# Regrouping the per-head matmuls of dilated attention between projection runs

## The chip, the cores and the metric

The kernel runs on one core of one Trainium2 chip. The metric is device time of one execution in microseconds; the median of several runs counts. The core's engines work side by side: TensorE (PE; its weight loads are PEld), VectorE (DVE), ScalarE (ACT), GpSimd (POOL) and SyncE (SP), which only issues DMAs here. Each takes its own instructions in order and waits on semaphores for the others.

## What is computed

A two-layer trunk over 512 tokens of width 1024: a state-space layer with its MLP, then an attention layer with its MLP. The change touches the attention alone. Sixteen heads of 64 have three branches each (window 128 at dilation 1, 512 at 4, 2048 at 16), and the outputs of the branches are mixed by the softmax of their log-sums. That mix equals one softmax over the keys of all three branches together, and so the kernel computes it.

```python
kv = (u @ w_kv).reshape(bsz, seq, 2, N_BRANCHES, N_HEADS, HEAD_DIM)
q = (u @ w_q).reshape(bsz, seq, N_BRANCHES, N_HEADS, HEAD_DIM)
for i, (win, dil) in enumerate(DILATED_BRANCHES):
    s = jnp.einsum('brnqhe,brnkhe->brnhqk', qb, k_band) * (HEAD_DIM ** -0.5)
    s = jnp.where(band_mask(nb, span), s, NEG)
    p = jnp.exp(s - max(s)); den = sum(p)
    o_i = einsum(p, v_band) / den; lse_i = max(s) + log(den)
o = sum_i softmax_i(lse)[i] * o_i
y = o @ w_o
```

## The kernel before

**Pairs and blocks.** Heads are taken in 8 pairs, a pair's queries in 4 blocks `qb` of 128. For one block TensorE does three small pieces of work. `attn_scores` (matmuls on L1107 and L1115) makes the scores of both heads in two PSUM buffers of the tag `aux`: 192, 384, 448 or 512 columns wide for blocks 0 to 3. Behind it stands the softmax: mask and maximum on VectorE (L1122, L1124), exponential on ScalarE (L1126), reciprocal and normalising on VectorE (L1129, L1131). `attn_turn` transposes the probabilities (L1142, L1144) and copies them to SBUF on both engines (L1147 to L1151). `attn_out` multiplies them by the values (L1163, L1170) into the pair's output tile `po`, which VectorE copies out when the pair is done (L1390).

**Projections as filler.** The q, k and v projections of later pairs, and a part of the output projection, come from a generator `feed`. Each step is three matmuls of 512 columns (L827, L828, L829: weights and activations are split in a high and a low part), or, for the values of the dilated branches, three of 256 columns (L1253 to L1255). A step yields its budgeted time: 0.64 us for three matmuls of 512 columns, 0.327 for the half as wide, 0.1 for a transpose. `fill(t)` runs steps until the budget t is used. One pair of q and k projections is KQ = 30.72, four heads' values are V = 32.77 (V counts 16 transposes, the generator makes 8). So `per`, a twelfth of what a pair takes from the feed, is 2.56 in even pairs and 5.29 in odd ones, 1.59 in pair 6 and 1.07 in pair 7. AHEAD is how far the feed is ahead of the heads when they begin, LEFT what stays for pair 7, REST what stays behind it.

**Order.** The order on TensorE is the program's order (`self.pinned(nc.tensor)`); on VectorE and ScalarE a planner places instructions by its own estimate of when they are ready, and each engine then runs them in that order. Per block the program has: transposes of this block, a fill of 1.4 per, scores of the next block, a fill of 1.6 per, value products of this block, and at once the transposes of the next.

**What else runs.** Weight blocks come by DMA three ahead. `weights` splits each in two halves: a cast on ScalarE (L799) and a subtraction on VectorE (L801), which, while heads run, are placed behind the exponential and the normalising pass of the latest scores in the program. In the first four pairs a gating job runs per block: `late_step` finishes the job at hand and issues four DMAs of 256 KB for the next, `late_half` does the next one's first half (L1494, then L1501). `split_o` splits a finished pair's output for the output projection (L1310, L1311), tied behind the same two passes.

Of the kernel before, what the change touches and what calls it, by code (L numbers as in the profile page):

```python
# [16 lines left out]
KT = D // P  # L17
# [15 lines left out]
PUMPS_END = ((0, 3), (1, 0), (1, 3))  # L33


AHEAD, LEFT, REST = 12.2, 11.6, 4.5

PARTS, PARTS_END = (1.4, 1.6, 0.0), (1.0, 1.0, 1.0)
NEG = -1e30


# [53 lines left out]
class Trunk:  # L95
# [1078 lines left out]
    def attention(self, adaq, adakv, gate):  # L1174
# [10 lines left out]
        kqs, vs, oparts = [None] * KT, [None] * 4, []  # L1185
# [119 lines left out]
        def split_o(k, cs=slice(0, T)):  # L1305
            if not any(uo):
                self.uo_tiles = self.uz_tiles()
            parts = [self.uo_tiles[k % 4][:, k // 4 * 2 + i] for i in range(2)]
            oh, ol = [x[:, cs] for x in parts]
            i = nc.scalar.copy(oh, ow[k][:, cs])  # L1310
            j = nc.vector.tensor_tensor(ol, ow[k][:, cs], oh.bitcast(F32), ALU.subtract)  # L1311

            self.after(i.ins, self.act_mark)
            self.after(j.ins, self.mark)
            uo[k] = parts
# [34 lines left out]
        def fill(t):  # L1350
            state[0] += t
            while state[0] > 0:
                c = next(steps, None)
                if c is None:
                    state[0] = 0.0
                    return
                state[0] -= c

        KQ, V = 6 * 8 * 0.64, 16 * 0.64 + 16 * 0.1 + 64 * 0.327
        with self.pinned(nc.tensor):  # L1360
            fill(0.327 * 15.5)
            self.pumped()
            self.table(AF.Exp, self.act_mark)
            fill(KQ + V + AHEAD - 9 * 0.64 - 0.327 * 15.5)
            self.heads = True
            nxt = self.attn_scores(0, kqs[0][0])
            fill(9 * 0.64)
            for pair in range(KT):

                per = (KQ + V * (pair % 2) - LEFT * (pair == KT - 2) if pair < KT - 1 else  # L1370
                       4 * 7 * 0.64 + LEFT - AHEAD - REST) / 12
                po = self.mm_ps()
                parts = PARTS if pair < KT - 1 else PARTS_END
                for qb in range(4):
                    pts = self.attn_turn(qb, nxt, kqs[pair][1])
                    fill(per * parts[0])
                    self.late_half()
                    if qb < 3:
                        nxt = self.attn_scores(qb + 1, kqs[pair][0])
                    elif pair < KT - 1:  # L1380
                        nxt = self.attn_scores(0, kqs[pair + 1][0])
                    fill(per * parts[1])
                    self.attn_out(pair, qb, pts, vs[pair // 2], po)

                    end = pair == KT - 1
                    if qb == 3 or end and qb == 2:
                        if ow[pair] is None:
                            ow[pair] = self.t([P, T], f"h{pair}")
                        bs = slice(3 if end and qb == 3 else 0, qb + 1)
                        nc.vector.tensor_copy(ow[pair].rearrange("p (b i r) -> p b r i", b=4, r=4)[:, bs],  # L1390
                                              po.rearrange("p (b r i) -> p b r i", b=4, r=4)[:, bs])
                        if end:
                            split_o(pair, slice(bs.start * P, bs.stop * P))
                    fill(per * parts[2])
                    self.late_step()
            fill(1000)
        self.heads = False
        self.table(AF.Sqrt, self.act_mark)
# [391 lines left out]
```

## Time and profile before

| what | us |
|---|---|
| median of 3 runs | 1551.63 (1550.26 to 1555.54) |
| the profiled execution's own time | 1551.77 |
| its span, first to last instruction | 1550.0 |
| TensorE matmuls busy over the span | 1464.0 (94%) |
| VectorE busy | 943.3 (61%) |
| ScalarE busy | 569.5 (37%) |
| the stretch of the attention heads | 694 to 1155 |

TensorE's matmuls are pipelined, so its busy share overstates how full it is: the distance from one start to the next start is the better measure, and the projections' 0.23 us is its steady state. In the rows below L12 is line 12 of the program and the arrow in brackets names what an engine waited for.

### The profile page before, as it was taken

To read this page: it belongs to the slowest core of one execution; us is meant where nothing else is said; L and a number is where in the kernel's file an instruction comes from. 1 tells how busy PE (TensorE), PEld (TensorE's weight loads), DVE (VectorE), ACT (ScalarE), POOL (GpSimd) and SP (SyncE) were. 2 spreads that over 40 slices of the span, in tenths; PEclk is the share of its full clock that TensorE was granted. 3 is DMA by queue.
4 is the path that set the end of the run, shared out by engine and by line. 5 is a ranking of instruction groups with operands and counts; after the bars stand their busy time and mean duration, and the time that the engine had idled before them with its cause. 6 is when DMAs were issued, how large, how long until landed. Compare 5 with 4: busy or idle time off the path is not lost. (4 is left out here: it accounts for less than half of the span.)

```text
span 1550.0 us, 27063 instructions
## 1 busy us (share of the span) xinstructions
PE 1464.0 (94%) x11540; PEld 1225.2 (79%) x11540; DVE 943.3 (61%) x1643; ACT 569.5 (37%) x990; POOL 134.1 (9%) x112
## 2 busy tenths in 40 slices
PE   2666999999999999999999999999999999999998
PEld 2445789888888888987987887898778888888887
DVE  8989996889884345635656756533558434344332
ACT  5566633413243233523322332332445423232222
POOL 8867200000000000100000000000000000000000
PEclk9687999999999999999999999999999999999999
DMA  9412580976643323233444445222334233232301
GB/s 219 147 56 78 159 254 28 301 242 204 208 159 109 108 88 123 59 107 114 138 126 142 139 116 157 71 67 56 116 104 137 82 109 108 83 109 82 109 1 55
DMA packets 214488, 188.59 MB, mean 122 GB/s; under 512 B 7480, under 2 KB 208352, under 8 KB 214368
## 3 DMA queue, kind: packets, MB, share of 16 engines
q1 hardware_dynamic: 214368, 186.87, 39.8%
q8 instruction: 90, 1.47, 0.4%
q14 instruction: 30, 0.25, 0.1%
HBM read 182.66 MB, written 4.19 MB: 121 GB/s over the span
## 5 line engine op out<-in xcount | busy, mean ns | idle before, releaser
L799 ACT CAST W<-W 128x1024 fp32r<-128x1024 f32 (+1 forms) x228 | 223.6, 1031 | 392.9 <-PE mm L828 201.8
L829 PE MATMUL mm<-uz,W 128*128 128x512 f32 (+1 forms) x952 | 358.1, 377 | 2.8 <-DVE W L801 2.8
L828 PE MATMUL mm<-uz,W 128*128 128x512 f32 (+1 forms) x952 | 357.8, 376 | 2.8 <-DVE uz L749 2.5
L827 PE MATMUL mm<-uz,W 128*128 128x512 f32 (+1 forms) x952 | 359.9, 380 | 0.2 <-ACT uz L1310 0.2
L801 DVE TENSOR_TENSOR W<-W,W 128x1024 fp32r<-128x1024 f32 (+1 forms) x228 | 266.6, 1197 | 151.1 <-ACT W L799 127.4
L827 PE MATMUL mm<-hid,W 128*128 128x512 f32 (+1 forms) x792 | 298.7, 378 | 0.9 <-ACT hid L1000 0.6
L828 PE MATMUL mm<-hid,W 128*128 128x512 f32 (+1 forms) x792 | 296.1, 374 | 2.7 <-DVE hid L1001 2.7
L829 PE MATMUL mm<-hid,W 128*128 128x512 f32 (+1 forms) x792 | 295.4, 373 | 0.0
L829 PEld LDWEIGHTS mm<-uz,W 128*128 128x128 f32 x952 | 179.7, 189 | 35.8 <-DVE W L801 3.2
L828 PEld LDWEIGHTS mm<-uz,W 128*128 128x128 f32 x952 | 179.7, 189 | 35.0 <-DVE uz L749 2.9
L827 PEld LDWEIGHTS mm<-uz,W 128*128 128x128 f32 x952 | 179.5, 189 | 34.0 <-ACT uz L1310 0.6
L828 PEld LDWEIGHTS mm<-hid,W 128*128 128x128 f32 x792 | 149.2, 188 | 29.4 <-DVE hid L1001 3.8
L827 PEld LDWEIGHTS mm<-hid,W 128*128 128x128 f32 x792 | 148.8, 188 | 28.8 <-issue 1.4
L829 PEld LDWEIGHTS mm<-hid,W 128*128 128x128 f32 x792 | 149.0, 188 | 26.6
L852 DVE SCALAR_TENSOR_TENSOR h<-mm,ada,h 128x512 f32<-128x512 f32 (+1 forms) x77 | 54.1, 708 | 148.4 <-PE mm L829 148.3
L1501 DVE SCALAR_TENSOR_TENSOR aacc<-W,cs,aacc 128x256 f32<-128x256 f32 x196 | 95.5, 487 | 4.0
L1029 DVE TENSOR_TENSOR sg<-sg 128x512 f32<-128x512 f32 x64 | 43.8, 688 | 55.5 <-ACT uz L1028 55.4
L1027 ACT ACTIVATE sg<-mm 128x512 f32<-128x512 f32 x60 | 35.6, 595 | 113.6 <-PE mm L829 112.0
L1253 PE MATMUL mm<-W,hid 128*128 128x256 f32 x256 | 73.5, 287 | 0.0
L1254 PE MATMUL mm<-W,hid 128*128 128x256 f32 x256 | 72.4, 283 | 0.0
L1255 PE MATMUL mm<-W,hid 128*128 128x256 f32 x256 | 72.4, 283 | 0.0
L1126 ACT ACTIVATE sg<-aux,st 128x192 f32<-128x192 f32 (+3 forms) x64 | 36.7, 577 | 96.1 <-DVE st L1124 96.1
(329 smaller groups left out, 1700.6 us busy)
## 6 DMA issues: line engine op xcount, KB each, us to landing
W<-in_mlp_w_dram SPq DMA_DIRECT2D x64, 1024.0 KB, 5.4
W<-in_ada_w_dram SPq DMA_DIRECT2D x20, 1024.0 KB, 7.2
h<-in_ada_w_dram SPq DMA_DIRECT2D x64, 256.0 KB, 3.2
W<-in_w_kv_dram SPq DMA_DIRECT2D x12, 1024.0 KB, 5.3
W<-in_w_kv_dram SPq DMA_DIRECT2D x24, 512.0 KB, 4.3
W<-in_attn_w_q_dram SPq DMA_DIRECT2D x24, 512.0 KB, 5.8
W<-in_ssm_w_glu_dram SPq DMA_DIRECT2D x16, 512.0 KB, 5.8
W<-in_kv_ada_w_dram SPq DMA_DIRECT2D x8, 1024.0 KB, 5.6
```

The source lines that it names most:

```text
L799: h = (nc.gpsimd.tensor_copy if first else nc.scalar.copy)(wh[:, ks], raw[:, ks])
L801: j = eng.tensor_tensor(wl[:, ks], raw[:, ks], wh[:, ks].bitcast(F32), ALU.subtract)
L827: nc.tensor.matmul(o, wh[:, k], uh, start=(start and k == order[0]), stop=False)
L828: nc.tensor.matmul(o, wh[:, k], ul, start=False, stop=False)
L829: self.pe_mark = nc.tensor.matmul(o, wl[:, k], uh, start=False, stop=(stop and k == order[-1])).ins
L852: self.mark = nc.vector.scalar_tensor_tensor(self.h[k][:, cs], src[:, cs], gate[:, k:k + 1], self.h[k][:, cs], ALU.mult, ALU.add).ins
L1029: nc.vector.tensor_tensor(rl, rl, rl, ALU.mult)
L1126: self.act_mark = nc.scalar.activation(p[:, 0:W], ps[:, 0:W], AF.Exp, bias=st[:, 1, e:e + 1], scale=0.125, accum_out=st[:, 2, e:e + 1]).ins
L1253: nc.tensor.matmul(ps[:, j], us[0], wh, start=(k == 0), stop=False)
L1254: nc.tensor.matmul(ps[:, j], us[0], wl, start=False, stop=False)
L1255: nc.tensor.matmul(ps[:, j], us[1], wh, start=False, stop=(k == KT - 1))
L1501: i = nc.vector.scalar_tensor_tensor(acc, raw[k], self.cs[:, k:k + 1], acc, ALU.mult, ALU.add)
```

## The change

The order of the three pieces is regrouped. Behind the scores of a block no longer stands one projection run, then its transposes. The loop now has groups: value products of block qb, transposes of block qb + 1, scores of block qb + 2, one behind the other with no projections between, then one fill and, at its end, `late_half`. `late_step` moves from behind the value products and their fill to right behind the scores. A pair has five groups: three with a fill of 3.2 per (the third without scores), then the value products of block 3 with the copy of `po` and the next pair's scores 0 (1.2 per), then the next pair's transposes 0 and scores 1 (1.2 per). Pair 6 has parts of its own (2.6, 2.6, 2.6, 2.1, 2.1), pair 7 has four groups. Before the loop pair 0 gets its first transposes, scores 1 and a fill of three steps. AHEAD goes from 12.2 to 15.0 and LEFT from 11.6 to 14.4, so `per` of pair 6 becomes 1.36 and that of pair 7 stays 1.07.

```diff
-AHEAD, LEFT, REST = 12.2, 11.6, 4.5
-PARTS, PARTS_END = (1.4, 1.6, 0.0), (1.0, 1.0, 1.0)
+AHEAD, LEFT, REST = 15.0, 14.4, 4.5
+PARTS, PARTS_6, PARTS_END = (3.2, 3.2, 3.2, 1.2, 1.2), (2.6, 2.6, 2.6, 2.1, 2.1), (3.2, 3.2, 3.2, 2.4, 0.0)
...
                 po = self.mm_ps()
-                parts = PARTS if pair < KT - 1 else PARTS_END
-                for qb in range(4):
-                    pts = self.attn_turn(qb, nxt, kqs[pair][1])
-                    fill(per * parts[0])
-                    self.late_half()
-                    if qb < 3:
-                        nxt = self.attn_scores(qb + 1, kqs[pair][0])
-                    elif pair < KT - 1:
-                        nxt = self.attn_scores(0, kqs[pair + 1][0])
-                    fill(per * parts[1])
-                    self.attn_out(pair, qb, pts, vs[pair // 2], po)
+                parts = PARTS if pair < KT - 2 else PARTS_6 if pair < KT - 1 else PARTS_END
+                if pair == 0:
+                    pts = self.attn_turn(0, nxt, kqs[0][1])
+                    nxt = self.attn_scores(1, kqs[0][0])
+                    fill(3 * 0.64)
+                for qb in range(5):
+                    if qb < 4:
+                        self.attn_out(pair, qb, pts, vs[pair // 2], po)
...
-                    fill(per * parts[2])
-                    self.late_step()
+                    if qb < 3:
+                        pts = self.attn_turn(qb + 1, nxt, kqs[pair][1])
+                    elif qb == 4 and not end:
+                        pts = self.attn_turn(0, nxt, kqs[pair + 1][1])
+                    if qb < 2:
+                        nxt = self.attn_scores(qb + 2, kqs[pair][0])
+                    elif qb > 2 and not end:
+                        nxt = self.attn_scores(qb - 3, kqs[pair + 1][0])
+                    if qb < 4:
+                        self.late_step()
+                    fill(per * parts[qb])
+                    if qb != 3:
+                        self.late_half()
```

## Rows read from the trace of the kernel before

**Rows 1.** Windows: length, busy us of PE, PEld, DVE, ACT, POOL, clock, DMA, GB/s.

```profile
693.00:1155.00 462.00, 455.97 (x5629) 376.96 (x5628) 256.63 (x608) 152.23 (x304) 0.00 (x0) 1.00 0.37 110
55.20:57.00 1.80, 1.80 (x16) 0.40 (x8) 1.80 (x1) 0.00 (x0) 1.50 (x1) 0.50 0.00 0
59.90:60.30 0.40, 0.40 (x12) 0.13 (x4) 0.36 (x2) 0.40 (x2) 0.40 (x1) 1.00 0.98 366
```

**Rows 2.** Waits of TensorE, 690 to 1160 us: total us, times, longest.

```profile
PE aux L1142 <- DVE sg L1131: 5.1, 5, 1.6
PE mm L828 <- DVE uz L1311: 0.4, 1, 0.4
PE mm L827 <- ACT W L1277: 0.3, 1, 0.3
PE mm L827 <- ACT uz L1310: 0.2, 1, 0.2
```

**Rows 3.** Timeline, TensorE, an undisturbed block: start, us, engine, line, operation, count.

```profile
799.02 0.39 PE L829 MATMUL mm<-uz,W 128*128 128x512 f32 x1
799.34 0.71 PE L1107 MATMUL aux<-W 64*128 64x128 f32 x8
...
800.58 0.50 PE L827 MATMUL mm<-hid,W 128*128 128x512 f32 x1
800.92 0.39 PE L828 MATMUL mm<-hid,W 128*128 128x512 f32 x1
801.15 0.39 PE L829 MATMUL mm<-hid,W 128*128 128x512 f32 x1
...
809.65 0.66 PE L1163 MATMUL mm<-W,W 128*64 128x128 f32 x8
...
811.78 0.47 PE L827 MATMUL mm<-uz,W 128*128 128x512 f32 x1
812.09 0.39 PE L828 MATMUL mm<-uz,W 128*128 128x512 f32 x1
```

**Rows 4.** Timeline, VectorE, four places: idle before and what ended it in brackets.

```profile
861.15 0.35 DVE L1494 TENSOR_SCALAR aacc<-h,cs 128x256 f32<-128x256 f32 x1 [1.81 <-DMA h<-in_ada_w_dram]
...
1112.50 2.36 DVE L801 TENSOR_TENSOR W<-W,W 128x1024 fp32r<-128x1024 f32 x2 [2.51 <-PE aux L1115]
...
1125.53 0.55 DVE L1131 TENSOR_SCALAR sg<-sg,st 128x192 f32<-128x192 f32 x2
...
1157.11 0.29 DVE L1311 TENSOR_TENSOR uz<-h,uz 128x128 fp32r<-128x128 f32 x1 [0.36 <-ACT uz L1310]
```

**Rows 5.** Timeline, TensorE, around pair 7's blocks 0 and 1.

```profile
1123.29 0.50 PE L827 MATMUL mm<-uz,W 128*128 128x512 f32 x1
...
1126.73 0.50 PE L828 MATMUL mm<-uz,W 128*128 128x512 f32 x1 [0.37 <-DVE uz L1311]
...
1131.85 0.50 PE L827 MATMUL mm<-uz,W 128*128 128x512 f32 x1
...
1135.33 0.38 PE L1142 MATMUL aux<-cst,sg 128*64 128x128 f32 x2
```

**Rows 6.** Timeline, TensorE, a block whose transposes wait.

```profile
866.12 0.66 PE L1163 MATMUL mm<-W,W 128*64 128x128 f32 x8
...
868.69 0.41 PE L1142 MATMUL aux<-cst,sg 128*128 128x128 f32 x2 [1.22 <-DVE sg L1131]
...
869.51 0.47 PE L827 MATMUL mm<-hid,W 128*128 128x512 f32 x1
```

**Rows 7.** Line 1494's waits, a gating job's first instruction: us, times.

```profile
  DMA h<-in_ada_w_dram: 42.3, 14
```

**Rows 8.** Instructions by line and shape: count, busy us, mean ns, idle before.

```profile
L1390 DVE COPY h<-mm 128x512 f32<-128x512 f32 x7 | 7.5, 1076 | 6.9 <-PE mm L1170 6.9
```

**Rows 9.** Timeline, TensorE, the same sixteen matmuls at either clock.

```profile
54.57 2.79 PE L282 MATMUL aux<-h,aacc 128*32 128x384 f32 x16
...
59.26 1.50 PE L282 MATMUL aux<-uz,aacc 128*32 128x384 f32 x16
```

## The prediction

> **What bounds the kernel now.** I read four views in this order. The windows say which engine is full and at which clock: over the attention heads, 693 to 1155 us, TensorE is busy 456 of 462 us at a granted clock of 1.00 (2.4 GHz), while VectorE is busy 257 and ScalarE 152 [rows 1]. So a microsecond is saved here only if TensorE starts its next matmul sooner. The amount of matmul work does not change; what can change is (a) the time TensorE waits for another engine and (b) the seams between unlike matmuls. For (a), TensorE's waits over that stretch [rows 2] are to be read as a list of everything that can be won: the transposes waited 5 times, 5.1 us in all, for the normalised probabilities, and 0.9 us went on three waits for copies and casts. No wait for a weight load or a weight split is among them. For (b), the timeline of an undisturbed block [rows 3] shows what a seam costs. For what makes the waits, the timeline of VectorE [rows 4] shows who stood ahead of the softmax in its queue.
>
> The heads run from a step budget: `fill(F)` issues projection steps of 0.64 (three matmuls) until F is used up. A step takes 3 x 0.23 = 0.68 us [rows 3], so a fill of F lasts about 1.06 F.
>
> **The waits that are there.** A block's chain is: scores, mask and maximum, exponential, normalising, transposes. Counted from the first projection behind the scores, undisturbed, it takes 2.7 us for block 0 (1123.29, to the end of the first half of the pass at 1125.53, and a start) and 3.5 us for block 1 (1131.85 to 1135.33) [rows 4, 5]; for block 3, with twice the columns or more, I take 4.2, an estimate from the same reading. Before, in an even pair (per = 2.56), the cover is 1.6 per plus the value products, 4.4 + 1.3 us (866.12 to 868.69 less 1.22 idle [rows 6]). That is enough unless something stands ahead on VectorE, and something does: the gating jobs' first instruction sat for its DMA 14 times, 42.3 us in all, 3.0 each [rows 7], and one of these at 861.15 is behind the wait at 868.69 [rows 4, 6]. In pair 6 it is a weight split that waited for the scores to release its buffer (1112.50), and that took 2 x 1.22 us ahead of block 3's maximum. So the 6.0 us are queueing on VectorE. Counted from start to start they are more, because each wait also costs a restart: the stalled group takes 869.51 - 866.12 = 3.39 us and the free one 811.78 - 809.65 = 2.13, which is 1.26 for 1.22 of idling [rows 3, 6]. The eight places together come to 6.9 us so counted.
>
> **Part 1: longer cover inside a pair.** Scores are now two groups ahead of their value products, and a fill of 3.2 per stands between scores and their transposes. Even pairs: 1.06 x 8.2 + 0.2 + 1.3 = 10 us against 4.2 needed; odd pairs 19; pair 7 (per 1.07): 5.1. A VectorE delay of 3 us no longer reaches TensorE in pairs 0 to 5. This removes 3.4 us of waits there (pair 0 block 3, pair 2 blocks 2 and 3); those of pairs 6 and 7 I also count as removed here, 3.5 us, and charge what comes back below. Sum **-6.9**.
>
> **Part 2: fewer seams.** A projection run pays at its ends: 0.09 for entering small matmuls (799.34 - 799.02 = 0.32 against 0.23), 0.11 for leaving scores (800.58 to 800.92) and 0.08 for leaving transposes (811.78 to 812.09), the latter mostly overlapped with the transposes, so I take 0.03 [rows 3]. A pair had eight runs and has five. Saved: three or four entries (0.3 us), three exits from transposes (0.1), one change from products to transposes (about 0.15). Added: three changes from transposes to scores and one from products to scores, which no row shows. The nearest is the entry to scores from full-height projections, 0.09; below it zero, above it 0.17, that of products to transposes. Taken: 0.09 x 3 + 0.15. Net 0.15 per pair, x7 = 1.0 (-0.9 to +3.4), and about 0.5 in pair 7, which goes from ten runs to four. Sum **-1.5** (+0.5 to -4).
>
> **Part 3: what is moved.** The second half of a job and the load of the next now stand right behind the scores, so the job's last instructions come behind the normalising pass; its four loads on SP's queue wait for that, and the weight loads behind them wait too. Those are three weights ahead, some 20 us, and no weight shows among the waits [rows 2], so nothing. The load has a whole fill, 8.7 us, to land instead of 1.4 per, but starts later; if it still holds VectorE, the inner groups hide it (5 us of slack). The larger AHEAD (+2.8) and the extra fill of 1.92 in pair 0 move projections forward without adding any: nothing. At the end, 0.4 units fewer remain to cover the last block's copy and split, which today finish at 1157.40 (1157.11 + 0.29) [rows 4], 2.7 us behind the last value products, four steps' worth. Cost 0 to 0.6, taken **+0.2**.
>
> **Part 4: where the new cover is thin.**
> - Pair 0's start: scores 1, then a fill of 1.92 and products 0: 2.0 + 0.2 + 1.1 = 3.3 us against 3.5: **+0.2**.
> - Each boundary behind an even pair: scores 0 of the next pair, then only 1.2 per, 3.3 + 0.2 = 3.5 us, against 2.7 plus 0.3, because the 1.08 us copy of the finished pair [rows 8] now stands ahead of the maximum. Slack 0.5. Then block 1: 3.5 + 1.1 against 3.5, slack 1.1, with the job's second half (2.1 us) and perhaps a split (2.4) on VectorE between. A hold of 3.0 us as in [rows 7] would cost 2.5 and 1.9. From 0 to 4.4 per boundary; I take a quarter of the middle, **+0.5** behind pairs 0 and 2 each, and 0 behind pair 4, where no job runs. Behind odd pairs the cover is 6.9 us: nothing.
> - Pair 6, block 3: the split that waits for the scores' buffer can again stand first: 4.2 + 2.4 against 1.06 x 3.5 + 0.2 + 1.3 = 5.3. From 0 to 1.3, taken **+0.7**.
> - Start of the output projection: its fourth step reads a split that is tied behind the latest normalising pass; today that costs the wait at 1126.73 [rows 5] and a smaller one 0.9 us before it, 1.0 in all. The generator's 8 transposes per quad are budgeted as 16, so by pair 6 the feed is 3 units ahead of the budget, and this step falls into the fill behind scores 0 of pair 7. From 0 to 1.5, taken **+1.0**.
> - Pair 7: cover 5.1 against 4.2, a split may come between: 0 to 2, taken **+0.3**.
>
> Sum: -6.9 - 1.5 + 0.2 + 0.2 + 1.0 + 0.7 + 1.0 + 0.3 = **-5.0 us**. The profiled execution took 1551.77 us (span 1550.0, 1.8 around it), so 1546.8; it stands 0.14 above the median of 1551.63, so **1546.6**, 0.32% less. Ends: -6.9 - 4 with no new wait, 1541; or all new waits at their upper ends, 1555.
>
> **The rivals.**
> - *The waits only move.* VectorE has the same work; what is lost inside a pair comes back at boundaries, in pair 6 and at the output projection. With half a boundary's 4.4 us behind pairs 0 and 2 and the upper ends in pair 6, the new waits are 0.2 + 4.4 + 1.3 + 1.5 + 0.3 + 0.2 = 7.9 in place of 3.4: -0.5, **1551**; a milder form, 5.4, gives **1548.6**. For it: the thin covers above. Against: three of five waits sat where cover becomes 10 us. Less than 0.3% (4.65 us, about what can be told from no change here) is this case. Chance 0.40.
> - *The boundary becomes the bound.* One mechanism: at an even pair's boundary VectorE has copy, two softmax chains, a job's halves and a split in 9 us, and a job's late load at the head of the queue holds them all. If it holds at both places of all three boundaries, 4.4 each, and splits do the same in pair 6 (2.8) and pair 7 (2): 13.2 + 4.8 + 0.6 - 8.4 = +10, **1562**. Break-even is at (8.4 - 2.4) / 3 = 2.0 us per boundary with the rest as taken; slower by 0.3% from 3.5. For it: 42.3 us of such holds. Against: longer time for each load, and pair 4 has no job. Chance 0.06.
> - *The clock falls.* Products, transposes and scores now stand together for 3.2 us without a projection. Today the clock stays at 1.00 over all heads, though a group with a wait lasted 3.39 [rows 1, 6]. At the low level sixteen small matmuls of one line took 2.79 us at a granted clock of 0.50 (1.2 GHz), and 1.50 us once it had risen to 1.00 [rows 1, 9]. If each of 16 long groups ran so, it would cost 16 x 3 = 48 us: 1600. Chance 0.02. The Trainium skill, page "TensorE: Matmul & The Clock Gate", section "Part 4: PE-mode transpose", says that transposes do not count as activity for the clock as matmuls do; by that rule the longer groups are a risk, and no group in this trace bears it out.
>
> **How the numbers follow.** The forecast has 0.52. Faster than 0.3%: 0.52; within: 0.40; slower: 0.08. The range takes in the forecast's better end and the first rival whole: 1542 to 1552.
>
> **What would show it.** In the changed kernel: in pairs 0 to 5, no wait of transposes inside a pair; waits only on the first and second transposes of pairs 1 and 3, and in pairs 6 and 7; five projection runs per pair; from transposes to scores about 0.1 us beyond the pitch; the clock at 1.00. It is wrong if boundary waits exceed 2 us each, if inner waits remain, or if that seam costs more than 0.2.

## The result and the profile after

The changed kernel takes 1566.6 us (1565.0 to 1567.4) where the kernel before takes 1553.1 (1550.3 to 1555.5) beside it: a ratio of 1.0087, with an interval of 1.0076 to 1.0099. It is slower by 13.5 us; 5 us less had been predicted, and the whole range lay below. The profiled execution has a span of 1563.4 us, against 1550.0 before.

In the kernel after, the lines named here have other numbers: the transposes wait on L1143 (L1142 before), the normalising pass is L1132 (L1131), the maximum L1123 (L1122), the exponential L1127 (L1126), a gating job's first instruction L1503 (L1494), the copy of the finished pair L1388 (L1390), the casts and subtractions of `split_o` L1311 and L1312 (L1310 and L1311). L1254 to L1256 are the value projections' matmuls (256 columns) and L1258 the copy that frees their PSUM buffer.

First the windows over TensorE (columns as in [rows 1]): the heads, one group with the run behind it, and two stretches further on.

```profile
693.00:1170.00 477.00, 461.61 (x5643) 385.81 (x5642) 261.41 (x609) 153.25 (x305) 0.00 (x0) 0.99 0.36 107
889.00:896.50 7.50, 7.45 (x151) 6.44 (x150) 3.71 (x11) 1.15 (x4) 0.00 (x0) 1.00 0.46 138
901.50:906.00 4.50, 4.46 (x21) 4.46 (x22) 3.00 (x6) 0.96 (x2) 0.00 (x0) 0.50 0.42 117
1139.20:1141.50 2.30, 2.23 (x5) 1.65 (x6) 1.21 (x3) 0.00 (x0) 0.00 (x0) 0.50 0.57 140
```

VectorE and ScalarE have nearly the same busy time as in [rows 1], and TensorE idles 15 us of the stretch instead of 6. The clock, 1.00 throughout before, is at 0.50 in two places. What TensorE waits for, over 600 to 1200 us (us in total, times, longest):

```profile
PE mm L1254 <- ACT W L1258: 6.5, 3, 5.1
PE aux L1143 <- DVE sg L1132: 5.0, 3, 2.6
PE mm L828 <- ACT uz L1311: 2.8, 1, 2.8
...
PE mm L829 <- DVE uz L1312: 1.0, 1, 1.0
```

Beside [rows 2] two things stand out. The transposes wait as long in sum as before, but at three places instead of five: 751.78 and 884.45, the boundaries behind pairs 0 and 2, and 1125.65, block 3 of pair 6. And the largest entry is one that [rows 2] doesn't have: a value projection waits for ScalarE to copy a PSUM buffer out. The place is the first group of pair 3. TensorE's timeline there (start, us, engine, line, operation, tiles, shape, count, idle before and what ended it):

```profile
884.45 0.38 PE L1143 MATMUL aux<-cst,sg 128*32 128x128 f32 x2 [2.64 <-DVE sg L1132]
...
889.63 0.44 PE L1164 MATMUL mm<-W,W 128*64 128x128 f32 x4
...
891.37 0.38 PE L1145 MATMUL aux<-cst,sg 128*128 128x128 f32 x2
891.68 0.71 PE L1108 MATMUL aux<-W 64*128 64x128 f32 x8
...
892.81 0.39 PE L1254 MATMUL mm<-W,hid 128*128 128x256 f32 x1
...
895.42 1.03 PE L1241 MATMUL mm<-cst,rstd 128*128 128x128 f32 x8
901.54 0.58 PE L1254 MATMUL mm<-W,hid 128*128 128x256 f32 x1 [5.09 <-ACT W L1258]
901.92 0.41 PE L1255 MATMUL mm<-W,hid 128*128 128x256 f32 x1
902.13 0.41 PE L1256 MATMUL mm<-W,hid 128*128 128x256 f32 x1
```

The group (products, transposes, scores) runs from 889.63 to 892.81 as planned. Then TensorE has 2.6 us of projections, 1.0 us of transposes of the values, and stops: its PSUM buffers are full. Why nobody empties them is on the two other engines. VectorE:

```profile
893.64 0.35 DVE L1503 TENSOR_SCALAR aacc<-h,cs 128x256 f32<-128x256 f32 x1 [3.24 <-DMA h<-in_ada_w_dram]
...
896.40 0.63 DVE L1123 CUSTOM_DVE_ANT_0 aux<-aux,bz 128x448 f32<-128x448 f32 x1
```

ScalarE:

```profile
897.79 0.63 ACT L1127 ACTIVATE sg<-aux,st 128x448 f32<-128x448 f32 x1 [5.58 <-DVE st L1125]
...
899.02 1.98 ACT L800 CAST W<-W 128x1024 fp32r<-128x1024 f32 x2
900.90 0.59 ACT L1258 COPY W<-mm 128x512 f32<-128x512 f32 x1
```

Read from below: the copy L1258 at 900.90 is what releases TensorE. It stands behind two weight casts (1.98 us), and these behind the exponential, which sat 5.58 us at the head of ScalarE's queue for the maximum. The maximum stands on VectorE behind the gating job, whose first instruction sat 3.24 us for its DMA. The last two of its four loads left SP's queue only from 887.66 on (the third of the last row below is the next job's), behind the end of the job before on VectorE (its last instruction, L1516, runs from 886.62 to 887.02) and behind two weight loads of 512 KB; no run parts the two. SP's queue:

```profile
881.71 3.61 SPq L1488 DMA_DIRECT2D h<-in_ada_w_dram  x2
885.37 0.46 SPq L790 DMA_DIRECT2D W<-in_w_kv_dram  x1
885.88 1.69 SPq L790 DMA_DIRECT2D W<-in_attn_w_q_dram  x1
887.66 8.49 SPq L1488 DMA_DIRECT2D h<-in_ada_w_dram  x3
```

So one late load, and the 2.3 us of the job's own instructions behind it, hold VectorE, VectorE holds ScalarE, and ScalarE holds a copy that has nothing to do with either. The loads as a whole do not hold VectorE longer than before. Its waits for them in the changed kernel (us, times), against 42.3 in 14 [rows 7]:

```profile
  DMA h<-in_ada_w_dram: 26.9, 12
```

What changed is what stands behind a hold.

The second stop with a low clock is the start of the output projection:

```profile
1132.59 0.50 PE L828 MATMUL mm<-uz,W 128*128 128x512 f32 x1
...
1137.74 0.50 PE L828 MATMUL mm<-uz,W 128*128 128x512 f32 x1 [2.82 <-ACT uz L1311]
1139.27 0.80 PE L829 MATMUL mm<-uz,W 128*128 128x512 f32 x1 [1.03 <-DVE uz L1312]
...
1141.56 0.63 PE L1143 MATMUL aux<-cst,sg 128*32 128x128 f32 x2
```

with ScalarE at that time:

```profile
1135.17 1.99 ACT L800 CAST W<-W 128x1024 fp32r<-128x1024 f32 x2 [0.44 <-DMA W<-in_attn_w_o_dram]
1137.07 1.65 ACT L1311 CAST uz<-h 128x512 fp32r<-128x512 f32 x3
```

Fifteen matmuls take 8.97 us (1132.59 to 1141.56) where fifteen at the full clock take 3.6 (0.34 for the first, then 0.23 each, [rows 3]). The split is tied behind pair 7's first softmax, and two weight casts that wait for their DMA stand between.

Counted from start to start, as the prediction counts, what TensorE loses in the heads is: 1.2 and 2.8 at the two boundaries, 1.3 in pair 6, 5.8 at the output projection (5.4 in the run, 0.4 in the group behind it, still at the low clock), and at the value projections 1.4, 5.3 and 0.5 plus 2.1 of low clock (23 steps from start to start, 901.92 to 906.83, of 0.213 instead of 0.120). That is 20.4 us in place of 6.9.

### The profile page after: what moved, and what is told of

It reads as the page before. It is cut to its first block, busy times and chain, and to the rows that moved or that the text cites. A ratio compares the mean times of both kernels' runs of the same rounds, so it can differ in the third digit from the quotient of the medians.

```text
span 1563.4 us, 27050 instructions
## 1 busy us (share of the span) xinstructions
PE 1466.1 (94%) x11540; PEld 1230.5 (79%) x11540; DVE 948.2 (61%) x1643; ACT 569.4 (36%) x990; POOL 134.9 (9%) x112
## 4 chain that ended last, share of the span: by engine, by line
PE 81%; DVE 12%; DMA 3%; issue 2%; ACT 1%; POOL 0%; SPq 0%; DVEq 0%; ACTq 0%
PE mm L828 23%; PE mm L829 23%; PE mm L830 22%; DMA h<-in_ada_w_dram 2%; PE mm L1254 2%; PE mm L1255 1%; PE mm L1256 1%; DVE aacc L1510 1%; PE mm L1171 1%; DVE W L802 1%; PE aux L1108 1%; PE aux L1143 1%; DVE W L705 1%; PE mm L1164 1%; DVE W L691 1%
## 5 line engine op out<-in xcount | busy, mean ns | idle before, releaser
L1254 PE MATMUL mm<-W,hid 128*128 128x256 f32 x256 | 74.8, 292 | 6.5 <-ACT W L1258 6.5
L1255 PE MATMUL mm<-W,hid 128*128 128x256 f32 x256 | 73.4, 287 | 0.0
L1256 PE MATMUL mm<-W,hid 128*128 128x256 f32 x256 | 73.3, 286 | 0.0
L1127 ACT ACTIVATE sg<-aux,st 128x192 f32<-128x192 f32 (+3 forms) x64 | 36.6, 577 | 93.4 <-DVE st L1125 93.4
```

The costliest lines, as they stand in the source:

```text
L1127: self.act_mark = nc.scalar.activation(p[:, 0:W], ps[:, 0:W], AF.Exp, bias=st[:, 1, e:e + 1], scale=0.125, accum_out=st[:, 2, e:e + 1]).ins
L1254: nc.tensor.matmul(ps[:, j], us[0], wh, start=(k == 0), stop=False)
L1255: nc.tensor.matmul(ps[:, j], us[0], wl, start=False, stop=False)
L1256: nc.tensor.matmul(ps[:, j], us[1], wh, start=False, stop=(k == KT - 1))
```

## The experiments

Each stands against runs of the kernel before on the same chip. In the table the difference is the ratio's, times 1552 us.

| kernel | us | ratio (interval) | difference |
|---|---|---|---|
| after | 1566.56 | 1.0087 (1.0076 to 1.0099) | +13.5 |
| e1_after_nojobs | 1555.61 | 1.0021 (1.0011 to 1.0031) | +3.3 |
| e2_before_nojobs | 1549.98 | 0.9986 (0.9976 to 0.9995) | -2.2 |
| e3_after_split6 | 1559.94 | 1.0047 (1.0032 to 1.0062) | +7.3 |
| e4_after_inner | 1564.14 | 1.0075 (1.0059 to 1.0091) | +11.6 |
| e5_after_none | 1545.82 | 0.9962 (0.9949 to 0.9975) | -5.9 |
| e8_split_vcopy | 1553.92 | 1.0011 (1.0002 to 1.0021) | +1.7 |
| e6_jobs_first | 1550.34 | 0.9989 (0.9979 to 0.9999) | -1.7 |
| e7_jobs_pool | 1569.72 | 1.0111 (1.0096 to 1.0126) | +17.2 |
| e9_jobs_odd | 1551.96 | 0.9996 (0.9987 to 1.0005) | -0.6 |
| e10_parts6 | 1551.51 | 0.9997 (0.9988 to 1.0006) | -0.5 |
| e11_before_both | 1551.64 | 0.9993 (0.9984 to 1.0002) | -1.1 |

**The gating jobs taken out of the changed kernel.** The 16 jobs with their loads and the small matmuls that close them are left out; the gates are a constant.

```diff
+        if late:
+            o = self.t([P, nk], f"ada{n}{c}")
+            nc.vector.memset(o, 0.25)
+            return o
```

> The changed kernel without the sixteen gating jobs of the attention stretch: their loads, their work on VectorE and their three closing matmul groups are left out, and the three gating vectors they make are set to a constant. Theory A, the job chain (a job's late load holds VectorE, the mask-and-maximum stands behind it, the exponential behind that, and on ScalarE the copies of the value projections behind the exponential, until TensorE idles 5 us and its clock halves): the waits behind pairs 0 and 2 (1.2 and 2.8 us), the waits of value matmuls (1.4, 5.3, 0.5) and the 2 us at the low clock go, some 13 us, so about 1553, and the granted clock stays at 1.00 up to pair 7. Theory B, the grouping itself (scores right ahead of a long run put exponentials and weight casts ahead of the value copies on ScalarE, jobs or not): the value waits stay, and only 2 to 4 us go, about 1563.

1555.6 us, between the two expectations: without the jobs the changed kernel is 10.2 us faster, though nearly all that they compute is on VectorE, which has time to spare. The edit takes their loads and their work away together, and no run here parts the two. The waits of TensorE that are left, same view as above:

```profile
PE mm L1254 <- ACT W L1258: 2.9, 3, 1.7
...
PE mm L828 <- ACT uz L1311: 2.2, 1, 2.2
...
PE aux L1143 <- DVE sg L1132: 1.2, 1, 1.2
```

Both boundary waits are gone; the one in pair 6 stays. So do the waits at the output projection, and a smaller part of those at the value projections. ScalarE shows why, at the same place as above:

```profile
888.29 0.64 ACT L1127 ACTIVATE sg<-aux,st 128x448 f32<-128x448 f32 x1 [2.16 <-DVE st L1125]
...
889.52 1.98 ACT L800 CAST W<-W 128x1024 fp32r<-128x1024 f32 x2
891.40 0.59 ACT L1258 COPY W<-mm 128x512 f32<-128x512 f32 x1
```

The queue is the same without a job: exponential, two casts, copy. The jobs make this queue late, but the order itself already costs 1.67 us of idling here.

**The jobs taken out of the kernel before.** The same four lines in the old order.

> The kernel before without the same jobs, left out in the same way. Theory A: the three transposes' waits of pairs 0 and 2 (3.4 us) go and little else, 1549 to 1550, so that the changed kernel without jobs stands 3 to 5 us above it (output projection +6.6, pair 6 about the same, seams -1.5). Theory B: the same here, and the gap to the changed kernel without jobs stays near 13.

1550.0 us: there the jobs cost 2.2 us. The same 16 jobs cost 10.2 in the new order. So 8.0 of the 13.5 us come from the jobs meeting the new order, and 5.5 (3.3 and 2.2) stand between the two orders without any job.

**The splits for the output projection earlier.** All six splits that it starts with are made in the last pair's projections, instead of three there and three from within the output projection's own steps.

```diff
-O_AHEAD = 3
+O_AHEAD = 6
```

> The changed kernel with O_AHEAD 6 in place of 3: all six splits that the first output projections read are made before the last keys, none behind pair 7's first scores. Theory C (the stall of 6 us at the start of the output projection is the casts and subtractions of these splits, tied behind pair 7's first softmax and a weight split that came late): 5 to 6 us less than the changed kernel, 1561, and no fall of the clock there. Rival: the output weights land late (their cast waited for the DMA until 1135.2), and that alone holds it: 0 to 2 us less.

1559.9 us, 6.2 less than after by the ratios (6.6 by the medians). The waits on `uz` are gone, while those of the other kind stay:

```profile
PE mm L1254 <- ACT W L1258: 6.7, 3, 5.5
...
PE aux L1143 <- DVE sg L1132: 4.8, 4, 2.1
```

So the start of the output projection, with its stretch at the low clock, costs what its start-to-start reading says, some 6 us, and what costs it is where the split stands in the order, not how long it takes.

**No job at the boundary behind an even pair.**

```diff
-                    if qb < 4:
+                    if qb < 3 + pair % 2:
                         self.late_step()
                     fill(per * parts[qb])
-                    if qb != 3:
+                    if qb < 3 or qb == 4 and pair % 2:
                         self.late_half()
```

> The changed kernel with the jobs kept but none at the boundary behind an even pair: jobs run in the three inner groups of every pair and in the fourth and fifth group of odd pairs only. Theory A: the boundary waits behind pairs 0 and 2 and the value waits behind them go, 8 to 13 us less than the changed kernel, 1554 to 1558. Theory B: no more than 4 us less.

1564.1 us, only 1.9 us better by the ratios, and the two intervals overlap. The boundary's wait behind pair 2 did not go; it became longer. The job ahead of the copy and the maximum there is the one whose first half stands behind the fill of the third group, and the edit leaves it in place. TensorE came 1.1 us earlier (the scores 0 at 876.19, after at 877.25), the load no earlier (879.21, after 879.00). VectorE, then TensorE:

```profile
879.21 0.35 DVE L1503 TENSOR_SCALAR aacc<-h,cs 128x256 f32<-128x256 f32 x1 [2.63 <-DMA h<-in_ada_w_dram]
...
881.78 0.36 DVE L1123 CUSTOM_DVE_ANT_0 aux<-aux,bz 128x192 f32<-128x192 f32 x1
```

```profile
884.63 0.38 PE L1143 MATMUL aux<-cst,sg 128*32 128x128 f32 x2 [3.87 <-DVE sg L1132]
...
1138.02 0.79 PE L828 MATMUL mm<-uz,W 128*128 128x512 f32 x1 [3.53 <-ACT uz L1311]
```

The job's first instruction still waits for its load, still ahead of the copy and the maximum that the boundary needs. Elsewhere the value projections' waits fell from 6.5 to 2.9 us, and a new one of 2.1 came at the small matmul that ends the gates. Taking the jobs out of two groups does not empty the boundary of the job that the group before them has begun.

**All three causes away.** No jobs, the splits early, and the value copies on VectorE, so that they don't stand behind a waiting exponential.

```diff
-O_AHEAD = 3
+O_AHEAD = 6
...
-                    nc.scalar.copy(vt[:, half * 2:half * 2 + 2], ps)
+                    nc.vector.tensor_copy(vt[:, half * 2:half * 2 + 2], ps)
...
+        if late:
+            o = self.t([P, nk], f"ada{n}{c}")
+            nc.vector.memset(o, 0.25)
+            return o
```

> The changed kernel without jobs (left out as before), with O_AHEAD 6, and with the copies of the dilated branches' values out of PSUM on VectorE instead of ScalarE. Theory A' (three causes that add: jobs holding VectorE, 11 us by the run without jobs; the splits of the output projection, 6.6 by the run with O_AHEAD 6; value copies behind exponentials and weight casts on ScalarE, 3.6 of waits that were left without jobs): 1555.6 - 6.6 - 3.6 = 1545 to 1546, that is 4 to 5 us below the kernel before without jobs, which is what the grouping itself would be worth. Rival B' (the grouping has a cost of its own that no wait shows): level with the kernel before without jobs, 1550, or above.

1545.8 us, as expected. Of TensorE's waits in the heads there remain:

```profile
PE aux L1143 <- DVE sg L1132: 1.2, 1, 1.2
...
PE mm L1254 <- DVE W L1258: 0.2, 1, 0.2
```

This is 3.7 us below the kernel before without jobs by the ratios (4.2 by the medians). It is not quite the grouping by itself: e2_before_nojobs lacks the two mends, which in the old order gain about 1.1 us, with an interval that takes in none (the last run below). So the grouping is worth some 2.6 to 3.7 us; the old order with both mends and no jobs was not run. The steps from after to here, 10.2 for the jobs and 9.2 for the two queues, make 19.4 us, and the list of losses read from the trace of after comes to 20.4, of which the 1.3 in pair 6 stays.

**With the jobs, the two queues mended.** The edit of the last kernel without its last part.

> The changed kernel with its jobs, O_AHEAD 6 and the value copies on VectorE. Theory A': against O_AHEAD 6 alone (1559.9) the waits of value matmuls (1.2, 5.5 and 0.5) and the low clock behind the second (2 us) go if ScalarE's queue was what held the copies: 1551 to 1553. Rival: the copies only stand behind the same held VectorE now, and 4 us or less is gained, 1556 to 1560.

1553.9 us, a little above the 1551 to 1553 expected: 11.8 of the 13.5 us come back, the value projections wait 1.6 us instead of 6.5 in idle time, and the transposes wait 4.8 us, four times. With both queues mended the jobs still cost 7.6 us (against all three causes away), and in the old order 2.2.

**The second half of a job ahead of the scores**, and with it the next load's issue, in the first three groups of a pair, beside the two mends:

```diff
+                    if qb < 3:
+                        self.late_step()
                     if qb < 2:
                         nxt = self.attn_scores(qb + 2, kqs[pair][0])
                     elif qb > 2 and not end:
                         nxt = self.attn_scores(qb - 3, kqs[pair + 1][0])
-                    if qb < 4:
+                    if qb == 3:
                         self.late_step()
```

> The same, and in the three inner groups the job's second half and the next load stand between the transposes and the scores instead of behind the scores, so that the load does not wait for the normalising pass. Theory A' (the late load is what holds VectorE): the job's DMA lands before its first instruction is reached, VectorE's waits for it fall from 27 us to under 12, and the time is 1547 to 1551. Rival: the second half, 2 us, now stands ahead of the maximum and the next transposes wait for it: no better than without this step.

1550.3 us, 0.1% below the kernel before: the lowest ratio of a kernel with all of the computation, though the intervals of the last three runs below overlap with its own. The time is as expected, the reason is not. The job's first instruction still waits, 20.2 us over 6 times where under 12 was expected; in e8_split_vcopy it was 19.6 over 10, so the loads hold VectorE no less than without this step. What went is the transposes' waits, 1.5 us in place of 4.8. One of the holds still reaches TensorE, now through VectorE's own value copy. Its row in the waits of VectorE's line, then VectorE's timeline, then TensorE's:

```profile
  DMA h<-in_ada_w_dram: 20.2, 6
```

```profile
888.48 0.35 DVE L1505 TENSOR_SCALAR aacc<-h,cs 128x256 f32<-128x256 f32 x1 [2.84 <-DMA h<-in_ada_w_dram]
...
894.29 0.65 DVE L1258 COPY W<-mm 128x512 f32<-128x512 f32 x1
```

```profile
895.00 0.39 PE L1254 MATMUL mm<-W,hid 128*128 128x256 f32 x1 [3.21 <-DVE W L1258]
```

**The jobs' products and sums on GpSimd**, which is idle in the heads, beside the two mends. VectorE keeps a job's transpose and its last sum.

```diff
-            i = nc.vector.tensor_scalar(acc, raw[0], self.cs[:, 0:1], None, ALU.mult)
...
-                i = nc.vector.scalar_tensor_tensor(acc, raw[k], self.cs[:, k:k + 1], acc, ALU.mult, ALU.add)
+                    e.tensor_scalar(raw[k], raw[k], self.cs[:, k:k + 1], None, ALU.mult)
+                    e.tensor_tensor(acc, acc, raw[k], ALU.add)
```

> O_AHEAD 6, value copies on VectorE, and the jobs' multiplications and additions on GpSimd (as a product and a sum, two instructions for one); only their transposes and reductions stay on VectorE. Theory A': with no job at the head of VectorE's queue that waits for a DMA, the time comes near the one without jobs, 1546 to 1549, below the kernel before. Rival: a job takes so long on GpSimd, or its transpose waits on VectorE for it, that VectorE is held as before: 1552 or more.

1569.7 us, slower than all others. VectorE waits for the loads no longer; it waits for GpSimd. GpSimd's instructions by line and shape (count, busy us, mean ns, idle before), the wait of VectorE over 690 to 1170 us, and what TensorE waits for:

```profile
L1509 POOL TENSOR_SCALAR h<-h,cs 128x256 f32<-128x256 f32 x112 | 121.3, 1095 | 19.9 <-DMA h<-in_ada_w_dram 19.8
L1510 POOL TENSOR_TENSOR aacc<-aacc,h 128x256 f32<-128x256 f32 x112 | 94.7, 846 | 7.8
```

```profile
DVE h L1524 <- POOL aacc L1510: 47.4, 10, 8.5
```

```profile
PE aux L1143 <- DVE sg L1132: 10.6, 5, 5.0
PE mm L1164 <- DVE W L1152: 4.8, 1, 4.8
```

A job takes seven rounds of 1.9 us on GpSimd. Its transpose on VectorE then sits at the head of the queue for up to 8.5 us, and what stands behind it is late. The cause is not the DMA as such but any instruction that waits at the head of VectorE's queue.

**Jobs shifted to the odd pairs**, where a group has twice the projections behind it: two per even pair and five per odd pair, on top of the order with the job's second half ahead of the scores.

```diff
+                    if qb < 2 or qb == 2 and (pair % 2 or pair == 4):
+                        self.late_step()
...
-                    if qb < 4:
+                    if qb > 2 and pair % 2:
                         self.late_step()
                     fill(per * parts[qb])
-                    if qb != 3:
+                    if qb < 2 or pair % 2 or pair == 4:
                         self.late_half()
```

> O_AHEAD 6, value copies on VectorE, the jobs' step between transposes and scores, and the sixteen jobs placed by room: two in the first two groups of an even pair, five in an odd pair, whose groups have twice the projections. If late loads at the even boundaries are what is left (the 3.2 us wait of value matmuls in the run with jobs first, and the waits of VectorE for job DMAs, 20 us in all there), both go and the time nears the one without jobs: 1546 to 1548. Rival: the odd pairs' boundaries now hold the same late loads, and the wait moves there: 1550 or more.

1552.0 us, not to be told from the kernel before. VectorE still waits 24.2 us over 9 times for the job's loads, where this was expected to go. The value projections' wait falls to 0.5 us, and two others take its place: one of the transposes in pair 7 (1.8 us of the 3.1 below), and the small matmul that ends the gates, since the last job ends later:

```profile
PE aux L1143 <- DVE sg L1132: 3.1, 2, 1.8
...
PE aux L1558 <- DVE apart L1518: 2.7, 1, 2.7
...
PE mm L1254 <- DVE W L1258: 0.5, 1, 0.5
```

**Other fills in pair 6**, a longer one behind its second group, which covers the third group's transposes, on top of that.

```diff
-PARTS, PARTS_6, PARTS_END = (3.2, 3.2, 3.2, 1.2, 1.2), (2.6, 2.6, 2.6, 2.1, 2.1), (3.2, 3.2, 3.2, 2.4, 0.0)
+PARTS, PARTS_6, PARTS_END = (3.2, 3.2, 3.2, 1.2, 1.2), (2.1, 3.7, 2.0, 2.1, 2.1), (3.2, 3.2, 3.2, 2.4, 0.0)
```

> The same with the fills of pair 6 at 2.1, 3.7, 2.0, 2.1, 2.1 in place of 2.6, 2.6, 2.6, 2.1, 2.1. If pair 6's wait of 1.4 us is a weight split standing ahead of block 3's maximum for 2.4 us, 1.5 us more projections behind these scores hide it: 1.0 to 1.5 us less than without, and no wait of transposes in pair 6. Rival: the split only follows the later scores' release of its buffer, or block 2's transposes wait in its place: no gain.

1551.5 us. Pair 6's wait of 1.3 is gone from the trace and the span is 1.2 us shorter, but the medians differ by 0.45, which the intervals can't tell from nothing.

**The two mends in the kernel before**, to see whether they are gains of their own: splits earlier, value copies on VectorE, in the old order.

> The kernel before with O_AHEAD 6 and the value copies on VectorE. If these two only mend what the grouping broke, the kernel before gains the 1.0 us at its own output projection at most: 1550.5 to 1552, and the run with jobs placed by room stands 3 to 5 us below it, which is then the grouping's own. Rival: the two edits help either order alike, and the grouping is worth nothing.

1551.6 us, 1.1 below the kernel before with an interval that takes in none. They are worth 11.8 us in the new order and about one in the old: what they mend was broken by the new order. The kernel with the jobs placed by room was to stand 3 to 5 us below this one and stands level with it (1552.0): with the jobs in, the grouping shows no gain.

## Why the prediction was wrong

**Part 1, the longer cover, was right.** In pairs 0 to 5 no transposes inside a pair wait any more; the three waits left stand where Part 4 had put them. **Part 2, the seams, holds where it was read.** From the transposes to the scores it is 0.31 us for two transposes of a pitch of 0.11 (891.37 to 891.68), so 0.09 beyond the pitch: the value taken. The other seams were not measured one by one. With no jobs on either side, 3.4 of the 6.9 us of waits are gone in the old order too (e2_before_nojobs keeps two of the five waits of transposes); the forecast's terms are then -3.5 and -1.5, and with the 1.3 that stayed in pair 6 they make -3.7, where e5_after_none stands at -3.7 by the ratios. That they meet so closely is luck, since either ratio's interval is 1.5 to 2 us to each side, and about 1 us of the 3.5 are the waits at the output projection.

**Part 3, "what is moved", failed first.** It priced the job's new place at nothing because the inner groups hide a hold on VectorE. They do hide it from the transposes, 10 us of cover to 4.2 needed. But the transposes are not the only thing that waits for VectorE: the exponential does, and it stands at the head of ScalarE's queue with the weight casts and the value projections' copies behind it. The prediction named who stands behind the job on VectorE, and did not go on to who stands behind the exponential on ScalarE. No row of before shows a value projection waiting: there the run behind the scores ended after 1.6 per, and a hold came out as a short wait of the transposes [rows 6]. After, the run behind the scores goes on for 3.2 per, and while it is made of value projections it needs a PSUM buffer freed again and again. The load, too, was given "a whole fill, 8.7 us, to land"; at the boundary it has two of 1.2 per, 3.3 us each, and the last of its issues stood behind the end of the job before. The term is 0 in the sum and measured 7.2 us from start to start plus 2.1 of low clock. The run without jobs puts the larger part of it on the jobs (these waits fall from 6.5 to 2.9 us, and the low clock behind them goes); the value copies on VectorE, with all else held, take 5.6 us off (e3_after_split6 against e8_split_vcopy).

**Part 4's terms, as they measured.** Start of pair 0: taken 0.2, no wait. Boundaries behind pairs 0 and 2: taken 0.5 each, measured 1.2 and 2.8, within the 0 to 4.4 given, the second beyond the 2 us that the prediction named as a sign of being wrong; a quarter of the middle was too little. Both vanish without jobs, so the mechanism is the one named, a job ahead of the maximum. At the second the load's lateness is 1.21 us of VectorE's idling (L1503 at 879.00 in the changed kernel), and the job's own instructions and the copy make up the rest. Pair 6: taken 0.7, measured 1.3, the upper end given; no experiment with the jobs out moved it, but a longer fill took it out of the trace, so it is the thin cover. Pair 7: taken 0.3, no wait of transposes.

**The start of the output projection is the second failed step.** The place and the tie were right ("its fourth step reads a split that is tied behind the latest normalising pass", "this step falls into the fill behind scores 0 of pair 7"); the size, 0 to 1.5, was carried over from the wait before, 1.0. In the new order that softmax is pair 7's first, which stands behind the copy of pair 6, and between softmax and split stand two casts of output weights (1.99 us) that wait for their DMA. It measured 5.8 us, of which some 1.6 is the low clock behind the waits (5.8 less 3.0 and 1.2 from start to start across the two), and taking the split out of that place returned 6.2.

**The sum with the measured terms.** With the seams as they were taken, -6.9 - 1.5 + 1.2 + 2.8 + 1.3 + 5.8 + 9.3 = +12.0 us, where the last term is the value projections'. The profiled spans differ by 13.4; 1.15 of that lies ahead of the heads, in work that the change doesn't touch (the same small matmuls of the norm ahead of the heads, L956 before and L957 after, start at 616.14 and at 617.29 us), and some 0.3 is not accounted for.

**The rivals.** "The boundary becomes the bound" had the larger cause right, a job at the head of VectorE's queue, with 8.0 of the 13.5 us, and its time, 1562, was the nearest of all. That nearness is luck, since its place was wrong: 4.0 us at the boundaries where it wanted 13. It got a chance of 0.06, because the case was thought to need all three boundaries; the stop that no term covered, and the one whose term was too small, brought the time without them. "The waits only move" holds for every later attempt: e4_after_inner, e6_jobs_first and e9_jobs_odd each took a wait away and got one elsewhere.

"The clock falls" came true in part, and not as told. The groups themselves run at 1.00: the window from 889 to 896.5 us holds one of 3.18 us. What went to 0.50 was the run behind a stop of TensorE, and those stretches vanish with the stops (e3_after_split6 shows a granted clock of 1.00 over 1100 to 1150, after 0.97). The Trainium skill, page "TensorE: Matmul & The Clock Gate", section "Part 4: PE-mode transpose", says that transposes do not count as activity for the clock the way matmuls do. No group of transposes, products and scores here lost the clock by itself (e5_after_none has all the groups, no stop above 1.3 us, and 1.00 over 693 to 1170). Behind a stop it is open: in e8_split_vcopy the clock fell within a boundary's group that came 1.95 us late.

**What stays open.** How to have both: the grouping is worth some 2.6 to 3.7 us, and with jobs no order tried here gets more than 1.7. At the place read above the last two of four loads left behind the end of the job before and behind two weight loads; loads into buffers of their own, free earlier, or ahead of the weights were not tried.

## What to carry to other kernels

When a cover is made longer for one consumer, follow every instruction behind the held one, on its engine and then on the engine that waits for it, until it ends at TensorE again: in order queues carry a hold to work that has no part in it. A reading of "no such wait in the trace" holds for the old order alone; a price of zero needs the reason why the new order keeps it so. When an order needs several mends to reach what it was before, test the order with the suspected disturbance removed on both sides, as e1_after_nojobs against e2_before_nojobs does: it tells the idea's worth from its collisions. Every mend made on one side belongs on the other too: e5_after_none has no such partner here, so its 3.7 us are not the grouping's alone.

## What the runs showed of the hardware

TensorE's clock did not survive every stop in the middle of full load, and the length of the stop alone does not tell which. Behind the waits of 5.09 us (901.54) and 3.53 us (1138.02 in e4_after_inner) the first matmul came at 1.2 GHz; behind 2.64 us (884.45) and 3.21 us (895.00 in e6_jobs_first) the run went on at 2.4 GHz. Shorter stops lost it: behind 1.95 us (883.74 in e8_split_vcopy) the transposes still ran at the full level and the scores behind them at the low one (granted clock 0.50 over 885 to 886 us), and behind 2.67 us (958.47 in e9_jobs_odd) it was 0.52 over 959 to 962 us. Behind 3.87 us (884.63 in e4_after_inner) the first small matmuls were at the full level and the next ones at the low. The stop at 1137.74, 2.82 us, was followed by a second of 1.03, and behind that the clock was low. Each of the two falls in the changed kernel cost 1.6 to 2.1 us on top of the stop that came before it.

GpSimd took 1095 ns for a product and 846 ns for a sum of 128 x 256 float32 numbers, and VectorE 0.48 us for both in one instruction: work that looks free on an idle engine was four times as long there, and its length came back as a wait.
